# FFN of a hybrid encoder layer: first layer by seven block products of eight, second layer in blocks of four tiles

## The chip, the cores and the metric

One core of a Trainium2 chip runs the whole kernel. The metric is device time in microseconds, the median of several executions; one more execution was profiled. TensorE (PE) multiplies; PEld is its weight load; VectorE (DVE), ScalarE (ACT) and GpSimd (POOL) do elementwise work; SyncE (SP) and ACT issue most transfers.

## The reference

One step of an encoder layer over 1024 prompt tokens and 8 x 16 sample tokens, 1152 in all, with 1024 channels. Three mixers come first; the change touches only what follows them:

```python
h = _layer_norm(DN_ALPHA * x + merged @ w_out, ln1_g, ln1_b)
f = jnp.square(jax.nn.relu(h @ w_ff1 + b_ff1)) @ w_ff2 + b_ff2      # 1024 -> 4096 -> 1024
y = _layer_norm(DN_ALPHA * h + f, ln2_g, ln2_b)
```

## The kernel before

Every float32 operand of a product is split into a rounded part and a remainder (`split`, L168 on POOL, L169 on DVE), and each product is three matmuls: high by high, high by low, low by high. All matmuls are recorded at L115 and all transposes at L120, so operations are told apart by their tiles.

The channel-major activations stay in two tiles, `xh` and `xl`, of 8 channel slices by 1152 tokens (`hh`, `hl` in `phase_out`). In `phase_out` the attention output is multiplied by `w_out` into nine token tiles `acc` of 128 x 1024. Each is normalised (`layer_norm`, L1319 to L1330), transposed on PE in two halves (`tp`), and written back to `hh` and `hl` (L1252, L1253).

The FFN then runs over 32 tiles of 128 hidden channels, in 16 blocks of two. For each tile `f`, `weights` loads two raw halves of `w_ff1` and splits them. `gemm` makes 24 matmuls of 384 columns for each of three token chunks, into the two banks `g` of PSUM. ACT applies bias, Relu (L1274) and Square (L1275), and POOL and DVE split the result into `uh`, `ul`. Two raw halves of `w_ff2` are split into `h2`, `l2`. After a block's two tiles the second layer runs: for each of nine token tiles and two halves of the output, 6 matmuls of 512 columns into a bank `op` (tag `o`, three banks), added to `acc` by DVE (L1298, L1300; L1304 in the last block). Behind the last block's sum each token tile is normalised and stored (L1313).

The order of instructions on each engine is fixed when the program is built. A list scheduler takes, by priority in program order, what its own estimate says is ready; on the chip each engine then runs its list in order. Tiles of a pool with `bufs=n` rotate over n buffers, and a pool that opens where a closed one lay waits, tile by tile, for what lay there.

Of the kernel before, what the change touches and what calls it, by code (L numbers as in the profile page):

```python
# [2 lines left out]

# [1 line left out]

# [6 lines left out]
F32 = mybir.dt.float32  # L12
F32R = mybir.dt.float32r
AF = mybir.ActivationFunctionType
ALU = mybir.AluOpType
# [4 lines left out]
P = 128  # L20
D = 1024
# [3 lines left out]
NT = SEQ + DB * DT  # L25
# [32 lines left out]
def run(g, n=-1):  # L58

    while n and next(g, g) is not g:  # L60
        n -= 1


class K:
# [66 lines left out]
    def setup(self):  # L131
        nc, d = self.nc, self.d
        nc.scalar.preload_act_table_set("natural_log_exp_and_others")
        cst = self.const.tile([P, C_END], F32, name="cst")
        self.cst = cst
        self.ident = cst[:, C_ID:C_ID + P]
        self.og = self.dram.tile([KT, P, NT], F32, name="og")
        self.started = set()

        self.gates = [(0, 0), (0, 1), (0, 2), (0, 3), (1, 7)] + [(2, t) for t in range(4)] + [(a, t) for t in range(4, KT) for a in (0, 2)]  # L140
        self.oa, self.oc, self.gb = (self.dram.tile([KT, P, NT], F32, name=n) for n in ("oa", "oc", "gb"))
        self.spq = self.dram.tile([KT, P, NT], F32, name="spq")
# [1075 lines left out]
    def phase_out(self, pool, ps):  # L1218
        nc, d = self.nc, self.d
        T9 = NT // P  # L1220
        hh, hl = self.xh, self.xl
        accs = [pool.tile([P, D], F32, name=f"acc{i}") for i in range(T9)]
        with self.pool("p2a") as pa:
            for i in range(6):
                nc.scalar.copy(accs[i][:, 0:512], self.early[i])
                nc.sync.dma_start(accs[i][:, 512:D], d["x"][i][:, 512:D])
            for i in range(6, T9):
                t = slice(i * P, (i + 1) * P)
                mg = pa.tile([P, KT, P], F32, name="mg", bufs=1)
                nc.sync.dma_start(mg, self.og[:, :, t].rearrange("k p n -> p k n"))  # L1230
                nc.scalar.copy(hh[:, :, t], mg)
                nc.vector.tensor_sub(hl[:, :, t], mg, hh[:, :, t].bitcast(F32))
                nc.sync.dma_start(accs[i], d["x"][i])
                run(self.out_mm(i, 0, self.w0, self.psg.tile([P, 512], F32, name="ps", tag="g"), accs[i][:, 0:512]))
            lng = pa.tile([P, 2, D], F32, name="lng")
            for i, n in enumerate(("ln1_g", "ln1_b")):
# [17 lines left out]
        self.right.close()  # L1254
        with self.pool("p2b") as pb:
            bf = pb.tile([P, NF], F32, name="bf")
            nc.sync.dma_start(bf, d["b_ff1"])
            lng = pb.tile([P, 2, D], F32, name="lng")
            bf2 = pb.tile([P, D], F32, name="bf2")
            for t, n in ((bf2, "b_ff2"), (lng[:, 0, :], "ln2_g"), (lng[:, 1, :], "ln2_b")):  # L1260
                nc.sync.dma_start(t, d[n].broadcast_to([P, D]))
            blk = 2
            for f0 in range(0, NF, blk):
                hid = []
                for f in range(f0, f0 + blk):
                    w = self.weights(d["w_ff1"][f].rearrange("p (k c) -> p k c", k=KT))
                    uh = pb.tile([P, NT], F32R, name="uh", bufs=3)
                    ul = pb.tile([P, NT], F32R, name="ul", bufs=3)
                    for c in range(NCH):
                        n = slice(c * CW, (c + 1) * CW)  # L1270
                        p = self.psg.tile([P, 512], F32, name="ps", tag="g")
                        run(self.gemm(p[:, :CW], w, hh, hl, c * CW, (c + 1) * CW))
                        r = pb.tile([P, CW], F32, name="r", bufs=2)
                        nc.scalar.activation(r, p[:, :CW], AF.Relu, bias=bf[:, f:f + 1])  # L1274
                        nc.scalar.activation(r, r, AF.Square)  # L1275
                        self.split(uh[:, n], ul[:, n], r)
                    w2 = []
                    for u in range(2):
                        raw = pb.tile([P, 512], F32, name="w2raw", bufs=3)
                        nc.sync.dma_start(raw, d["w_ff2"][f][:, u * 512:(u + 1) * 512])  # L1280
                        h2 = pb.tile([P, 512], F32R, name="h2", bufs=6)
                        l2 = pb.tile([P, 512], F32R, name="l2", bufs=6)
                        self.split(h2, l2, raw)
                        w2.append((h2, l2))
                    hid.append((uh, ul, w2))
                last = f0 + blk == NF
                for i in range(T9):
                    t = slice(i * P, (i + 1) * P)
                    for u in range(2):
                        o = ps.tile([P, 512], F32, name="op", tag="o", bufs=3)  # L1290
                        m = 0
                        for uh, ul, w2 in hid:
                            for a, b in ((uh, w2[u][0]), (uh, w2[u][1]), (ul, w2[u][0])):
                                self.mm(o, lhsT=a[:, t], rhs=b, start=m == 0, stop=m == 3 * blk - 1)
                                m += 1
                        a = accs[i][:, u * 512:(u + 1) * 512]
                        if f0 == 0:
                            nc.vector.scalar_tensor_tensor(a, a, ALPHA, o, op0=ALU.mult, op1=ALU.add)  # L1298
                        elif not last:
                            nc.vector.tensor_add(a, o, a)  # L1300
                        else:
                            if u == 0:
                                sm = pb.tile([P, 2], F32, name="sm", bufs=2)
                            nc.vector.tensor_tensor_reduce(out=a, in0=o, in1=a, scale=1.0, scalar=0.0, op0=ALU.add, op1=ALU.add, accum_out=sm[:, u:u + 1])  # L1304
                    a = accs[i]
                    if f0 == blk:
                        nc.gpsimd.tensor_add(a, a, bf2)
                    if last:
                        self.layer_norm(pb, a, sm, lng, hl[:, :, t], i >= T9 - 2)
                        m = 2 if i >= T9 - 2 else 1  # L1310
                        for u in range(m):
                            v = slice(u * D // m, (u + 1) * D // m)
                            nc.sync.dma_start(d["o_y"][i][:, v], a[:, v])  # L1313

    def layer_norm(self, pool, a, s, gb, jk, short=False):

# [100 lines left out]
```

## Time and profile before

| | us |
|---|---|
| median of 3 executions | 2750.88 (2748.21 to 2756.87) |
| the profiled execution | 2752.38 |
| its span, first to last instruction | 2750.5 |
| FFN, first matmul of 384 columns to the end | about 1928 to 2750.5 |

In the rows, "mean ns" or min/median/max is the duration of one instruction. Matmuls overlap, so what one costs in a dense run is the distance from start to start. A row of the chain gives start, length and how many instructions were merged into it. A row of a timeline may end with the idle time before it and what ended it.

### The profile page before, as it was taken

The numbers are of one execution on the slowest core, as the hardware profiler recorded it, in microseconds if no ns is written. First come the engines' busy times: TensorE is split into PE (matmuls) and PEld (weight loads), VectorE is DVE, ScalarE is ACT, GpSimd is POOL, SyncE is SP. The second block draws the span as 40 slices with busy tenths as digits, with TensorE's granted clock in tenths as the row PEclk, the third lists the DMA queues.
The fourth block names the chain that finished last, engine by engine and source line by source line (L and its number), as shares of the span: only waits on it lengthen the run. The fifth ranks groups of instructions, "written<-read, shape, count | busy, mean of one in ns | idle before, by whom it ended". The sixth has DMA issues, their size and how long they took to land.

```text
span 2750.5 us, 45013 instructions
## 1 busy us (share of the span) xinstructions
PE 2655.3 (97%) x16361; PEld 2464.2 (90%) x16361; DVE 1448.3 (53%) x3353; ACT 1004.5 (37%) x2749; POOL 809.3 (29%) x1197
## 2 busy tenths in 40 slices
PE   8999999999999989999989989999999999999997
PEld 7989999999999989888888888878999999999996
DVE  4647484755647563333556666555444444444445
ACT  5646474655647453223433333234211111111113
POOL 2222222222222222212645555323251211211213
PEclk9999999999999999999999999999999999999999
DMA  6343434434343434444866766561210110110101
GB/s 224 104 153 120 163 123 149 148 125 164 114 150 120 163 124 148 164 155 153 252 180 199 211 196 185 175 218 47 79 57 31 54 39 31 54 39 31 61 20 69
DMA packets 263261, 343.27 MB, mean 125 GB/s; under 512 B 55408, under 2 KB 188160, under 8 KB 260480
## 3 DMA queue, kind: packets, MB, share of 16 engines
q1 hardware_dynamic: 201344, 245.93, 28.5%
q10 hardware_dynamic: 61696, 94.47, 10.0%
q8 instruction: 129, 2.11, 0.3%
q14 instruction: 92, 0.75, 0.1%
HBM read 267.69 MB, written 105.13 MB: 136 GB/s over the span
## 4 chain that ended last, share of the span: by engine, by line
PE 81%; DMA 8%; DVE 5%; issue 3%; POOL 2%; ACT 1%; SPq 0%; ACTq 0%; DVEq 0%; POOLq 0%
PE ps L115 48%; PE op L115 16%; PE od L115 3%; PE S L115 3%; PE t L115 2%; PE tb L120 2%; PE sc L115 1%; PE tp L120 1%; PE kk L115 1%; DMA bv<-spn 1%; DVE tmp L786 1%; PE o L115 1%; DMA wraw<-in_w_mem 1%; PE ob L115 1%; DMA kb<-in_cak 1%
## 5 line engine op out<-in xcount | busy, mean ns | idle before, releaser
L115 PE MATMUL ps<-xh,whi 128*128 128x384 f32 x2712 | 950.3, 350 | 10.3 <-POOL whi L168 7.0
L115 PE MATMUL ps<-xh,wlo 128*128 128x384 f32 x2712 | 927.6, 342 | 1.8 <-DVE wlo L169 1.8
L115 PE MATMUL ps<-xl,whi 128*128 128x384 f32 x2712 | 927.3, 342 | 0.0
L115 PEld LDWEIGHTS ps<-xh,whi 128*128 128x128 f32 x2712 | 511.2, 189 | 27.7 <-POOL whi L168 7.0
L115 PEld LDWEIGHTS ps<-xl,whi 128*128 128x128 f32 x2712 | 511.1, 188 | 16.5 <-issue 5.0
L115 PEld LDWEIGHTS ps<-xh,wlo 128*128 128x128 f32 x2712 | 510.2, 188 | 10.0 <-issue 2.5
L1300 DVE TENSOR_TENSOR acc<-op,acc 128x512 f32<-128x512 f32 x252 | 174.0, 691 | 276.2 <-PE op L115 276.1
L168 POOL TENSOR_SCALAR whi<-wraw 128x512 fp32r<-128x512 f32 x261 | 181.4, 695 | 458.2 <-PE ps L115 381.8
L1274 ACT ACTIVATE r<-ps,bf 128x384 f32<-128x384 f32 x96 | 55.6, 581 | 664.7 <-PE ps L115 659.7
L169 DVE TENSOR_TENSOR wlo<-wraw,whi 128x512 fp32r<-128x512 f32 x261 | 194.1, 744 | 163.2 <-POOL whi L168 161.2
L115 PE MATMUL op<-h,uh 128*128 128x512 f32 x576 | 225.6, 392 | 1.2 <-DVE sm L1304 1.2
L115 PE MATMUL op<-h,ul 128*128 128x512 f32 x576 | 226.1, 392 | 0.0
L115 PE MATMUL op<-l,uh 128*128 128x512 f32 x576 | 225.5, 392 | 0.0
L168 POOL TENSOR_SCALAR uh<-r 128x384 fp32r<-128x384 f32 x96 | 55.0, 573 | 491.8 <-ACT r L1275 479.9
L372 POOL TENSOR_SCALAR pt<-pt,sta 128x640 f32<-128x640 f32 (+3 forms) x144 | 111.3, 773 | 278.3 <-DVE sta L371 231.5
L618 DVE SCALAR_TENSOR_TENSOR y<-z,wc,y 128x384 f32<-128x384 f32 (+1 forms) x216 | 132.2, 612 | 28.2 <-ACT y L615 18.3
L115 PEld LDWEIGHTS op<-h,ul 128*128 128x128 f32 x576 | 108.2, 188 | 23.9
L115 PEld LDWEIGHTS op<-h,uh 128*128 128x128 f32 x576 | 108.3, 188 | 19.5 <-DVE sm L1304 2.0
L370 ACT ACTIVATE pt<-pt,sta 128x640 f32<-128x640 f32 (+3 forms) x144 | 101.0, 701 | 64.6 <-DVE sta L369 53.3
L115 PEld LDWEIGHTS op<-l,uh 128*128 128x128 f32 x576 | 108.1, 188 | 15.5
L368 DVE CUSTOM_DVE_ANT_0 pt<-S,tab 128x640 f32<-128x640 f32 (+4 forms) x128 | 83.7, 654 | 52.4 <-PE S L115 38.5
L169 DVE TENSOR_TENSOR ul<-r,uh 128x384 fp32r<-128x384 f32 x96 | 53.6, 560 | 102.0 <-POOL uh L168 102.0
(374 smaller groups left out, 4562.4 us busy)
## 6 DMA issues: line engine op xcount, KB each, us to landing
wraw<-in_w_in SPq DMA_DIRECT2D x160, 256.0 KB
kb<-in_cak SPq DMA_DIRECT2D x16, 1024.0 KB
vb<-in_cav SPq DMA_DIRECT2D x16, 1024.0 KB
wraw<-in_w_ff SPq DMA_DIRECT2D x64, 256.0 KB
w2raw<-in_w_ff SPq DMA_DIRECT2D x64, 256.0 KB
o_aks<-in_cak ACTq DMA_DIRECT2D x32, 496.0 KB
o_avs<-in_cav ACTq DMA_DIRECT2D x32, 496.0 KB
spn<-kn ACTq DMA_DIRECT2D x48, 192.0 KB
```

The lines of the kernel that those rows point to most:

```text
L115: ins = self.nc.tensor.matmul(out, **kw)
L120: ins = self.nc.tensor.transpose(out, **kw)
L168: nc.gpsimd.tensor_scalar(hi, raw, 1.0, 0.0, op0=ALU.mult, op1=ALU.add)
L169: nc.vector.tensor_sub(lo, raw, hi.bitcast(F32))
L368: nc.vector.tensor_tensor_reduce(out=P_, in0=S, in1=tab, scale=1.0, scalar=-3e38, op0=ALU.add, op1=ALU.max, accum_out=st[:, 0:1])
L370: nc.scalar.activation(P_, P_, AF.Exp, bias=st[:, 1:2], accum_out=st[:, 2:3])
L372: nc.gpsimd.tensor_scalar(P_, P_, st[:, 3:4], 0.0, op0=ALU.mult, op1=ALU.add)
L618: nc.vector.scalar_tensor_tensor(y[:, :w], z[:, i:i + w], wc[:, i:i + 1], y[:, :w], op0=ALU.mult, op1=ALU.add)
L786: nc.vector.tensor_tensor(tmp[:, 0:t, 0:t], y[:, 0:t, 0:t], m[:, 0:t, t].unsqueeze(1).broadcast_to([72, t, t]), op=ALU.mult)
L1274: nc.scalar.activation(r, p[:, :CW], AF.Relu, bias=bf[:, f:f + 1])
L1300: nc.vector.tensor_add(a, o, a)
```

## The change

The first four tiles of the first layer are computed as before, in four chunks of 288 columns instead of three of 384. The other 28 go in 14 pairs. For a pair, the tokens (two halves of 576), the input channels (two halves of four slices) and the two tiles form a 2 x 2 block product, which is made from seven block products instead of eight (Winograd's form). A product has 24 matmuls of 288 columns, in two banks. The sums of activations (S1 to S4) are made once by DVE and POOL from an unrounded copy `hm` and split by ACT and DVE; S3 takes the place of the upper half of `hh`. The sums of weights (t1 to t4) are made by POOL for each pair, and the products are added up by DVE out of PSUM. The PSUM banks rotate over three tags.

The hidden activations no longer stay on chip: each goes to DRAM (`hid`) and is read back by the second layer, which starts when the first is through, in 8 blocks of four tiles. Its `uh`, `ul` lie in the 8 slices of `xh`, `xl`. The nine `acc` also go to DRAM (`hd`) and come back. Raw weights of both layers share six buffers. `layer_norm` gets a scratch tile `jk`.

```diff
+        self.hd = self.dram.tile([NT // P, P, D], F32, name="hd")
+        self.hid = self.dram.tile([NF, 2, P, NT // 2], F32, name="hid")
...
+            hm = self.on_right("hm").tile([P, KT, NT], F32, name="hm")
...
+                nc.scalar.dma_start(self.hd[i], a)
...
                     nc.scalar.copy(hh[:, s, t], v)
+                    nc.scalar.copy(hm[:, s, t], v)
...
+        with self.pool("p2n") as pn:
+            raw = lambda: pn.tile([P, 512], F32, name="raw", bufs=6)
+            uraw = pn.tile([P, 2, NT], F32, name="uraw")
+            with self.pool("p2b") as pb:
+                self.ffn1(pb, ps, hm, raw)
+            self.right.close()
+            with self.pool("p2c") as pb:
+                self.ffn2(pb, ps, raw, uraw)
+    def ffn1(self, pool, ps, hm, raws):
+        bf = pool.tile([P, NF], F32, name="bf")
...
+        S = {i: tuple(pool.tile([P, 4, H], F32R, name=f"s{i}{n}") for n in "hl") for i in (2, 1, 4)}
+        S[3] = hh[:, top, two], hl[:, top, two]
+        names = cycle("gtogto")
...
+        def hidden(r, f, i):
+            nc.scalar.activation(r, r, AF.Relu, bias=bf[:, f:f + 1])
+            nc.scalar.activation(r, r, AF.Square)
+            nc.scalar.dma_start(self.hid[f, i], r)
...
+        for k in range(4):
+            a11, a21, a12, a22 = [hm[:, q, n] for q in (k, 4 + k) for n in (one, two)]
+            nc.vector.tensor_add(a22, a21, a22)
+            nc.gpsimd.tensor_sub(a21, a11, a21)
+            nc.vector.tensor_sub(a11, a22, a11)
+            self.cast(S[2], k, a11)
+            self.cast(S[1], k, a22)
+            self.cast(S[3], k, a21)
+            nc.vector.tensor_sub(a12, a12, a11)
+            self.cast(S[4], k, a12)
+        pool = self.on_right("p2r")
+        A11, A12, A22 = [(hh[:, q, n], hl[:, q, n]) for q, n in ((top, one), (low, one), (low, two))]
+        for f in range(4, NF, 2):
...
+            def product(a, raw):
+                w = [self.wp.tile([P, 4, P], F32R, name=n, tag=n, bufs=4) for n in ("whi", "wlo")]
+                self.split(*w, raw)
+                banks = []
+                for j in range(2):
+                    banks.append(bank())
+                    for k in range(4):
+                        for m, (x, y) in enumerate(((0, 0), (0, 1), (1, 0))):
+                            self.mm(banks[j], lhsT=w[x][:, k, :], rhs=a[y][:, k, half(j)], start=k == m == 0, stop=k == 3 and m == 2)
+                return banks
+            def add(x, banks):
+                y = keep()
+                for j in range(2):
+                    nc.vector.tensor_add(y[:, half(j)], banks[j], x[:, half(j)])
+                return y
+            p1 = keep()
+            for j, b in enumerate(product(A11, R[0, 0])):
+                nc.scalar.copy(p1[:, half(j)], b)
+            hidden(add(p1, product(A12, R[1, 0])), f, 0)
+            nc.gpsimd.tensor_sub(t1, R[0, 1], R[0, 0])
+            nc.gpsimd.tensor_sub(t2, R[1, 1], t1)
+            u2 = add(p1, product(S[2], t2))
+            u4 = add(u2, product(S[1], t1))
+            nc.gpsimd.tensor_sub(t4, R[1, 0], t2)
+            u5 = add(u2, product(A22, t4))
+            nc.gpsimd.tensor_sub(t3, R[1, 1], R[0, 1])
+            hidden(add(u4, product(S[4], R[1, 1])), f + 1, 0)
+            b = product(S[3], t3)
+            hidden(add(u5, b), f, 1)
+            hidden(add(u4, b), f + 1, 1)
+    def cast(self, pair, k, src):
+        self.nc.scalar.copy(pair[0][:, k, :], src)
+        self.nc.vector.tensor_sub(pair[1][:, k, :], src, pair[0][:, k, :].bitcast(F32))
+    def ffn2(self, pb, ps, raws, uraw):
+        blk = 4
+        for f0 in range(0, NF, blk):
+            for f in range(f0, f0 + blk):
+                raw = uraw[:, f % 2, :]
+                nc.sync.dma_start(raw.rearrange("p (i n) -> p i n", i=2), self.hid[f].rearrange("i p n -> p i n"))
+                uh, ul = self.xh[:, (f + 4) % 8, :], self.xl[:, (f + 4) % 8, :]
+                for c in range(NCH):
+                    n = slice(c * CW, (c + 1) * CW)
+                    self.split(uh[:, n], ul[:, n], raw[:, n], "act")
+                for u in range(2):
+                    raw = raws()
+                    nc.sync.dma_start(raw, d["w_ff2"][f][:, u * 512:(u + 1) * 512])
+                    h2 = pb.tile([P, 512], F32R, name="h2", bufs=12)
+                    l2 = pb.tile([P, 512], F32R, name="l2", bufs=12)
+                    self.split(h2, l2, raw)
...
+            if f0 == 0:
+                accs = [pb.tile([P, D], F32, name=f"acc{i}") for i in range(T9)]
...
+                for i in range(T9):
+                    nc.sync.dma_start(accs[i], self.hd[i])
```

What follows in `ffn2` (a block's matmuls for each token tile and half, now 12 over four tiles where it was 6 over two, the sum into `acc`, the last block's `layer_norm` and stores) has the text of before.

## Rows read from the trace of the kernel before

**Rows 1.** Page, part 1: busy us, share of the span, instructions of each engine.
```profile
PE 2655.3 (97%) x16361; PEld 2464.2 (90%) x16361; DVE 1448.3 (53%) x3353; ACT 1004.5 (37%) x2749; POOL 809.3 (29%) x1197
```

**Rows 2.** Windows (busy of PE, PEld, DVE, ACT, POOL; clock; DMA share; GB/s): block, last block, tail.
```profile
2142.67:2192.91 50.24, 50.24 (x253) 45.70 (x253) 21.96 (x33) 6.63 (x12) 9.65 (x15) 1.00 0.13 42
...
2710.14:2736.30 26.16, 24.98 (x109) 19.78 (x107) 22.89 (x45) 17.97 (x36) 12.81 (x6) 1.00 0.22 89
2736.30:2750.48 14.18, 0.11 (x1) 0.00 (x0) 10.09 (x15) 4.95 (x10) 5.01 (x2) 0.64 0.43 169
```

**Rows 3.** Chain that ended last (start, us, what), FFN: both kinds of matmul.
```profile
2142.67 14.84 PE ps L115 x84
2157.51 4.10 PE op L115 x18
```

**Rows 4.** Timeline of PE, two stretches of narrower matmuls (start us, us, instruction).
```profile
139.87 0.31 PE L115 MATMUL S<-kd,qs 128*128 128x320 f32 x1
...
140.44 0.28 PE L115 MATMUL od<-pth,vv 128*128 128x256 f32 x1
...
1127.52 0.36 PE L115 MATMUL ps<-memh,whi 128*128 128x256 f32 x1
1127.72 0.28 PE L115 MATMUL ps<-meml,whi 128*128 128x256 f32 x1
...
1138.92 0.28 PE L115 MATMUL ps<-memh,wlo 128*128 128x256 f32 x1
```

**Rows 5.** Tile memh: weight loads of 256-column matmuls (ns min/median/max).
```profile
L115 PEld LDWEIGHTS ps<-memh,whi x128: 187/190/194, 1070.0 to 1253.6; 128*128 128x128 f32 x128
```

**Rows 6.** Groups by shape, whole span: DVE, POOL and ACT operations nearest the new ones.
```profile
L169 DVE TENSOR_TENSOR l<-w2raw,h 128x512 fp32r<-128x512 f32 x64 | 56.9, 910 | 12.2 <-POOL h L168 12.2
L169 DVE TENSOR_TENSOR ul<-r,uh 128x384 fp32r<-128x384 f32 x96 | 53.6, 560 | 102.0 <-POOL uh L168 102.0
L833 DVE TENSOR_TENSOR at<-kk,E 128x256 f32<-128x256 f32 x24 | 10.1, 422 | 20.4 <-PE kk L115 20.4
...
L168 POOL TENSOR_SCALAR h<-w2raw 128x512 fp32r<-128x512 f32 x64 | 49.7, 778 | 70.9 <-PE op L115 46.5 <-DMA w2raw<-in_w_ff 23.2
L991 POOL TENSOR_TENSOR we<-wv,cst 128x512 f32<-128x512 f32 x16 | 18.1, 1133 | 3.4 <-DMA o_ssmp<-S 1.7 <-ACT wv L979 1.2 <-PE kk L115 0.4
...
L1275 ACT ACTIVATE r<-r 128x384 f32<-128x384 f32 x96 | 50.3, 525 | 2.9
```

**Rows 7.** Timeline of ACT in the first normalisation.
```profile
1916.14 1.15 ACT L1320 ACTIVATE xl<-acc,lst 128x1024 fp32r<-128x1024 f32 x1 [2.31 <-issue]
```

**Rows 8.** Tile acc on DVE, last 51 us (ns min/median/max, first and last start).
```profile
L1304 DVE CUSTOM_DVE_ANT_0 acc<-op,acc x18: 673/680/692, 2711.6 to 2738.5; 128x512 f32<-128x512 f32 x18
L1321 DVE SCALAR_TENSOR_TENSOR acc<-acc,lst,lng x9: 1272/1286/3196, 2715.2 to 2743.3; 128x1024 f32<-128x1024 f32 x9
L1327 DVE SCALAR_TENSOR_TENSOR acc<-acc,lst,lng x4: 737/739/740, 2744.5 to 2746.5; 128x512 f32<-128x512 f32 x4
```

**Rows 9.** Timeline of the tail: PE's last matmul, ACT, and SP's stores.
```profile
2736.02 0.39 PE L115 MATMUL op<-h,ul 128*128 128x512 f32 x1
...
2740.08 1.13 ACT L1320 ACTIVATE xl<-acc,lst 128x1024 fp32r<-128x1024 f32 x1
...
2741.21 0.47 ACT L1322 ACTIVATE lst<-lst,eps 128x1 f32<-128x1 f32 x2
...
2740.04 7.56 SPq L1313 DMA_DIRECT2D o_y<-acc  x6
```

**Rows 10.** Timeline: a 512 KB load issued by SP, and ACT's first read of it.
```profile
1842.73 0.38 SPq L1230 DMA_DIRECT2D mg<-og  x1
...
1846.92 1.04 ACT L1231 CAST xh<-mg 128x1024 fp32r<-128x1024 f32 x1
```

**Rows 11.** Page, part 2: GB/s in 40 slices of the span.
```profile
GB/s 224 104 153 120 163 123 149 148 125 164 114 150 120 163 124 148 164 155 153 252 180 199 211 196 185 175 218 47 79 57 31 54 39 31 54 39 31 61 20 69
```

More of the change, by code (lines that the diff above doesn't have):

```diff
@@ L1 @@
 from contextlib import ExitStack, contextmanager
-from itertools import chain
+from itertools import chain, cycle
 import numpy as np
@@ L1221, in phase_out @@
         hh, hl = self.xh, self.xl
-        accs = [pool.tile([P, D], F32, name=f"acc{i}") for i in range(T9)]
         with self.pool("p2a") as pa:
+            accs = [pa.tile([P, D], F32, name=f"acc{i}") for i in range(T9)]
             for i in range(6):
@@ L1252, in phase_out @@
                     nc.scalar.copy(hh[:, s, t], v)
+                    nc.scalar.copy(hm[:, s, t], v)
                     nc.vector.tensor_sub(hl[:, s, t], v, hh[:, s, t].bitcast(F32))
[L1254 to L1286, printed above, removed]
-                for i in range(T9):
[L1288 to L1313, printed above, removed]
@@ new lines, in phase_out, with bank @@
+        with self.pool("p2n") as pn:
[7 more added lines that the diff above has]
+    def ffn1(self, pool, ps, hm, raws):
+        nc, d = self.nc, self.d
+        hh, hl = self.xh, self.xl
+        H = NT // 2
+        bf = pool.tile([P, NF], F32, name="bf")
+        nc.sync.dma_start(bf, d["b_ff1"])
+        one, two = slice(0, H), slice(H, NT)
+        top, low = slice(0, 4), slice(4, 8)
+        S = {i: tuple(pool.tile([P, 4, H], F32R, name=f"s{i}{n}") for n in "hl") for i in (2, 1, 4)}
+        S[3] = hh[:, top, two], hl[:, top, two]
+        names = cycle("gtogto")
+        def bank():
+            tag = next(names)
+            if tag == "g":
+                return self.psg.tile([P, 512], F32, name="ps", tag="g")[:, 0:288]
+            return ps.tile([P, 512], F32, name=tag + "p", tag=tag, bufs={"t": 2, "o": 3}[tag])[:, 0:288]
+        def hidden(r, f, i):
+            nc.scalar.activation(r, r, AF.Relu, bias=bf[:, f:f + 1])
+            nc.scalar.activation(r, r, AF.Square)
+            nc.scalar.dma_start(self.hid[f, i], r)
+        res = lambda: pool.tile([P, H], F32, name="r", bufs=3)
+        for f in range(4):
+            w = self.weights(d["w_ff1"][f].rearrange("p (k c) -> p k c", k=KT))
+            for i in range(2):
+                r = res()
+                for j in range(2):
+                    p = bank()
+                    run(self.gemm(p, w, hh, hl, (2 * i + j) * 288, (2 * i + j + 1) * 288))
+                    u = r[:, j * 288:(j + 1) * 288]
+                    nc.scalar.activation(u, p, AF.Relu, bias=bf[:, f:f + 1])
+                nc.scalar.activation(r, r, AF.Square)
+                nc.scalar.dma_start(self.hid[f, i], r)
+        for k in range(4):
[11 more added lines that the diff above has]
+        for f in range(4, NF, 2):
+            R = {}
+            for g in range(2):
+                src = d["w_ff1"][f + g].rearrange("p (k c) -> p k c", k=KT)
+                for q in range(2):
+                    R[q, g] = raws().rearrange("p (k c) -> p k c", k=4)
+                    nc.sync.dma_start(R[q, g], src[:, 4 * q:4 * q + 4, :])
+            t1, t2, t3, t4 = (pool.tile([P, 4, P], F32, name="tsum", bufs=6) for _ in range(4))
+            half = lambda j: slice(288 * j, 288 * j + 288)
+            keep = lambda: pool.tile([P, H], F32, name="keep", bufs=5)
+            def product(a, raw):
[10 more added lines that the diff above has]
+                y = keep()
+                for j in range(2):
+                    nc.vector.tensor_add(y[:, half(j)], banks[j], x[:, half(j)])
[15 more added lines that the diff above has]
+            hidden(add(u4, b), f + 1, 1)
```

38 lines of the change are left out of this document (added).

## The prediction

> **What bounds the kernel now.** I read the busy times first. TensorE is busy 97% of the span, DVE 53%, POOL 29% [rows 1], but a share of busy time over the span says little of one stage, so next came windows of the FFN. In a block of two hidden tiles PE is busy 50.24 of 50.24 us at the full granted clock (1.00, the 2.4 GHz level), while DVE works 22 us, POOL 10 and ACT 7 [rows 2]. The chain of waits agrees: through the FFN it is matmuls alone, one after the other [rows 3]. So here a matmul removed is time removed, and the other engines have more than half of their time free. From the chain come the prices of a matmul in a dense run: 14.84/84 = 176.7 ns at 384 columns and 4.10/18 = 227.8 ns at 512 [rows 3]. A block is 144 x 0.1767 + 108 x 0.2278 = 50.05 us, so the rows leave 0.2 us of it unexplained. Only the end is different. In the last block PE has matmuls in flight for 24.98 of 26.16 us, and after its last one come 14.2 us in which DVE, ACT, POOL and a store end the program [rows 2].
>
> **The seven products.** Before, a pair of hidden tiles costs 144 x 0.1767 = 25.44 us. After, it has 7 x 24 = 168 matmuls of 288 columns, a shape that the trace doesn't show. The nearest rows on either side are 256 columns, where a dense run goes from 1127.72 to 1138.92, 94 steps of 119 ns, and 320 columns, four in 0.57 us, 143 ns each [rows 4]. These are the bounds: between 119 and 143 ns. A line from 119 at 256 to 176.7 at 384 gives 148 at 320, so it is some 5 too high there, and 133.4 at 288; halfway between the two bounds is 131. I take 133, near the line, since its operands are those of the 384-column run. A pair then costs 168 x 0.133 = 22.34 us, 3.10 less, and 14 pairs save **43.4 us**. The bounds for it are 14 x (25.44 - 168 x 0.119) = 76 and 14 x (25.44 - 168 x 0.143) = 20. An eighth of the 356 us of these pairs would be 44.5; narrower matmuls carry a larger fixed part.
> The Trainium skill, "TensorE: Matmul & The Clock Gate", section "Back-to-back issue gap", puts a single warm gap at N/2.4 + 2.5 ns, 122.5 ns for 288 columns. By that the pairs would save 14 x (25.44 - 20.58) = 68 us. The row of 384 columns is 176.7 where the same rule says 162.5, so the row decides.
>
> The first four tiles keep their columns in four chunks: 384 x 0.133 = 51.07 us against 288 x 0.1767 = 50.89, **+0.2 us**. The second layer has the same 1728 matmuls of 512 columns, so nothing changes on PE; its DVE sums halve in number, which are off the path.
>
> **What the other engines get in a pair of 22.3 us.** DVE: seven remainders at up to 0.910, and 14 sums of 288 columns from PSUM at about 0.455 (between 0.422 at 256 and 0.560 at 384): 12.7 us. POOL: seven roundings at 0.778 and four weight sums at 1.133: 10.0 us. ACT: eight passes over 576 columns at about 0.71 (from 0.525 at 384 [rows 6] and 1.15 at 1024 [rows 7]), two copies and four transfers to issue at some 0.4 each: 7.3 us [rows 6]. All is hidden by PE. Uncovered, DVE's work beyond today's would be the dearest. Weight tiles have four buffers and products use six banks in turn, so PE can be three products (9.6 us) ahead of what empties them. Transfers: a pair loads 1.05 MB and stores 1.18, 100 GB/s; a second-layer block of 49.2 us loads 4.5 MB, 90 GB/s. Earlier slices of the span move up to 252 [rows 11]. I cost them at nothing.
>
> **Making the sums of activations.** Per channel slice DVE has three sums and four remainders of 576 columns (about 0.8 each, by 0.560 at 384): 22 us for four slices; ACT 16 casts at 0.71, 11 us; POOL four differences at about 1.3. They start when the last token tile is transposed and are hidden by the 51 us of the first four tiles. S3 alone must wait until those have read the upper half of `hh`. It then takes four casts and four remainders, pipelined some 4 us, and the weight sums lie where `hm` lay, so POOL's t1 and t2 (2.3 us) and a split (1.7) come behind: 8 us against two products (6.4 us) that PE can do before the third. In `phase_out` each token tile gives ACT two more copies (0.6 each) and a transfer that waits for POOL's last sum; behind it stand the next tile's Square and copies. ACT idles 2.31 us per tile there [rows 7], so 1.6 fits; if it doesn't, PE has tiles 0 to 3 of earlier tokens to go on with. For all this **+1 us**, bounds 0 and 8.
>
> **The turn from the first layer to the second.** It didn't exist before, since the layers alternated. Call T the end of the last product. The second layer's first four tiles go into the lower slices of `xh`, free for good after the fifth product, at T - 6.3. The hidden tiles come through two buffers, so the third can only be loaded when the first is split (two more chunks on ACT and DVE, about 1.6 us, T - 4.7). A load of 0.5 MB takes 4.2 us from issue to use [rows 10], and one more split 1.1: T + 0.6 for tile three, about T + 2 for tile four, where PE wants them at T + 1.4 and T + 2.1. Also, the first `h2` lies where the bias `bf` and S2 lay, and `bf` is read by the last Relu: two DVE sums, then ACT, then a split, about T + 4. PE can do the other output half first if the list has it so. The nine `acc` come back behind on SP's queue; the first sum needs one at about T + 4. I take **+3 us**. Below: 0, all covered. Above: all four tiles split after T, one load and 12 x 0.56 + 8 x 0.91, 18 us.
>
> **The tail.** Before, the last block gives a token tile 2.73 us of PE, while DVE needs two sums (0.76 each with the read of the sum), 0.2 and 1.27 to 3.2 us for the fused normalisation; the last two of the nine queue up [rows 8]. From PE's last start at 2736.02 to 2750.5 are 14.5 us. After, a tile has 5.47 us of PE, so DVE keeps up. What is left behind the last matmul: 0.4 to its end, 0.76 + 0.4, Square and its read 1.3, two small passes 0.5, two halves at 0.74, and 3.2 for the last store (from 2747.3, the last half's end, to 2750.5): 8.0 us [rows 8, 9]. With 1.3 us of stall inside the last block (26.16 against 108 x 0.2278 = 24.6 and the last one's end): **-7.7 us**, bounds -9 and -4.
>
> **Sum.** 2752.4 (the profiled execution, 1.5 above the median of the runs and within them) - 43.4 + 0.2 + 1 + 3 - 7.7 = 2705.5. I forecast **2705 us**.
>
> **The rivals.**
> *The turn is serial.* If the list has the splits in an order that the chip can't use, the upper bound above holds, 15 us more: 2715 to 2725. For it speaks that two hidden buffers and `bf` tie the start to the end of the first layer; against it, that the first chunks are free at T - 16.
> *Products wait.* A matmul whose group had to wait shows 200 ns to the next one instead of 119 (from 1127.52) [rows 4]. If every half product began so, 196 x 0.08 = 16 us; if each product also waited 0.3 us for a weight or a bank, 98 x 0.3 = 29 more: 2721 to 2750. DVE can be slowed by POOL: the same normalisation took 1.27 and 3.2 us [rows 8]. If DVE were lengthened by all of POOL's four sums, 12.7 + 4.5 = 17.2 us, still under 22.3. So waits would come from order, not from load. From 0.5 us per product the gain is gone.
> *Weight loads bind.* This one ends slower. PEld is busy 45.7 of 50.24 us of a block [rows 2], 91%, and the change raises the loads: 276 instead of 252 per pair of tiles over both layers, and 96 more in the first four. If a load's slot of 50.24/252 = 0.199 us set the pace, 14 x 24 + 96 = 432 loads more are 86 us: 2835. It decides from 151 ns per matmul of 288 columns, where a pair costs what it did. Against it: loads of 187 to 194 ns each [rows 5] run beside 256-column matmuls that start every 119 ns [rows 4], so loads overlap one another.
> The Trainium skill, "Perfetto Trace Analysis", section "Identifying the Most-Contended Engine", judges TensorE's headroom by the busy share of LDWEIGHTS; by it the loads are nearly full here, and 2835 would be the time. The 256-column rows speak against.
>
> **How the numbers follow.** Chances: forecast 0.70, serial turn 0.10, products wait 0.15, loads bind 0.05. A time within 0.3% (8 us) of before is what a measurement of this kernel can't tell from no change. The first two are faster; of the third 0.07 ends below 2743, 0.05 in between, 0.03 above; the fourth is slower. So faster 0.87, same 0.05, slower 0.08. The forecast's own range: the line was about 5 ns off at 320 columns, and 6 ns on 2352 + 384 matmuls is 16 us either way, 2689 to 2721. The serial turn and the milder waits add the stretch up to 2730. So 2689 to 2730.
>
> **What would show it.** Right: matmuls of 288 columns start 130 to 136 ns apart with no idle PE between products; 22 to 23 us per pair; a hole of 0 to 5 us where the layers meet; about 8 us from the last matmul to the end. Wrong: steps of 140 ns or more; idle PE before product groups put down to POOL or DVE; a hole of over 10 us at the turn, or a lower clock behind it; a second layer with gaps where a block begins.

## The result, and the profile after

The changed kernel takes 2714.14 us (median, 2710.72 to 2718.88, four executions), the kernel before, run beside it, 2753.88. The ratio is 0.987 (95% interval 0.9853 to 0.9886): 1.3% faster, 36 us by the ratio (31 to 40). The forecast was 2705, with a range from 2689 to 2730. The profiled execution took 2710.72 us with a span of 2708.9.

Busy times, page of the kernel after, part 1, the line that answers to [rows 1]. PE has 432 matmuls more and is busy 48 us less:

```profile
PE 2607.6 (96%) x16793; PEld 2418.9 (89%) x16793; DVE 1494.4 (55%) x3475; ACT 1063.6 (39%) x2851; POOL 866.9 (32%) x1203
```

Windows of the kernel after, columns as in [rows 2]: more than eleven pairs of the seven products; the turn between the layers; a stretch of the third second-layer block; 49 us of a later block; the tail from the last matmul's start.

```profile
2016.12:2275.69 259.57, 259.57 (x1958) 259.57 (x1958) 128.97 (x247) 74.15 (x122) 108.56 (x124) 1.00 0.29 101
...
2286.70:2303.50 16.80, 4.53 (x10) 2.86 (x10) 11.70 (x22) 9.17 (x19) 4.84 (x6) 0.63 0.91 305
...
2409.50:2418.00 8.50, 5.20 (x16) 3.83 (x15) 6.54 (x13) 1.29 (x3) 0.05 (x1) 0.80 0.81 254
...
2463.00:2512.00 49.00, 49.00 (x218) 40.56 (x217) 25.03 (x38) 5.96 (x13) 6.89 (x8) 1.00 0.29 93
...
2700.40:2708.90 8.50, 0.34 (x2) 0.00 (x0) 4.00 (x7) 1.74 (x4) 0.00 (x0) 0.72 0.33 124
```

In the products PE is busy 259.57 of 259.57 us at clock 1.00: 259.57/1958 = 132.6 ns a matmul. The last block and its tail [rows 2] took 26.16 + 14.18 us; from the last matmul's start to the end it is now 8.6. New are two holes, in the second and third window, where PE works 4.53 of 16.80 and 5.20 of 8.50 us, at mean granted clocks of 0.63 and 0.80. The chain of waits, start, length and what, is matmuls alone in the products and in a later block (as in [rows 3]), and at the turn it leaves PE:

```profile
2016.12 1.58 PE ps L115 x12
2017.70 1.60 PE tp L115 x12
2019.30 1.58 PE op L115 x12
...
2280.42 3.65 DMA uraw<-hid
...
2286.16 3.76 DMA uraw<-hid
...
2290.48 2.34 DVE xl L171 x3
...
2292.84 5.26 DMA uraw<-hid
...
2298.12 0.52 ACT xh L166
...
2298.66 1.50 DVE xl L171 x3
2300.16 0.61 DVE l L171
...
2300.79 6.59 DMA raw<-in_w_ff
...
2307.45 0.62 POOL h L170
...
2439.85 60.29 PE op L115 x266
...
2700.88 0.60 DVE acc L1416
...
2701.84 1.25 ACT jk L1432 x2
...
2703.11 1.30 DVE acc L1433
...
2704.50 0.75 DVE acc L1439
2705.25 0.66 DVEq L1519
```

How long each stage took, by the starts of its matmuls (PE's timeline, first and last of each shape), in us:

| stage | before | after |
|---|---|---|
| `phase_out` from the first `op<-woh` matmul to the FFN's first | 1862.0 to 1927.6: 65.6 | 1851.9 to 1917.5: 65.6 |
| FFN, first matmul to the start of the last | 808.4 | 782.8 |
| the last matmul's start to the end | 14.5 | 8.6 |
| together | 888.5 | 857.0 |

The part that the change touches became 31.5 us shorter. The two profiled executions differ by 41.7: the other 10 us lie ahead of `phase_out`, in instructions that the change leaves as they were. In eleven more executions, of this kernel and of variants, `phase_out` begins between 1859.7 and 1870.9, so 1851.9 was an early one. All stage times below count from a matmul, which leaves this out.

Pure matmuls explain most of it: before 16 x 25.44 + 1728 x 0.2278 = 800.6, after (2352 + 384) x 0.133 + 393.6 = 757.5. That is 43.1 less. What exceeds the pure matmuls grew from 7.8 to 25.3 us. After, 5.2 of it are in the first layer and 20.3 in the second (counted to the last matmul's end, 0.2 more), of which 16.2 lie in its first block, 5.0 in its third, and nearly nothing in the others.

Where the 16.2 come from is seen in PE's timeline at the turn, kernel after (a bracket holds the idle time before, and what ended it):

```profile
2286.53 0.29 PE L115 MATMUL tp<-xh,wlo 128*128 128x288 f32 x1
2290.58 0.50 PE L115 MATMUL op<-h,xh 128*128 128x512 f32 x1 [3.76 <-POOL h L170]
...
2291.57 1.22 PE L115 MATMUL op<-h,xh 128*128 128x512 f32 x2 [0.49 <-POOL h L170]
...
2300.82 0.80 PE L115 MATMUL op<-l,xh 128*128 128x512 f32 x1 [8.02 <-DVE l L171]
2301.41 0.63 PE L115 MATMUL op<-h,xl 128*128 128x512 f32 x1
2301.84 0.63 PE L115 MATMUL op<-h,xh 128*128 128x512 f32 x1
```

Two waits, for the first rounded weight `h` and for the first remainder `l`. Behind the second, matmuls start 427 ns apart instead of 227, at a granted clock of 0.50 (the 1.2 GHz level), which lasts until 2304.8; the 0.63 above is the mean of both levels. A window inside that stretch:

```profile
2301.40:2303.50 2.10, 2.10 (x6) 1.67 (x5) 2.10 (x5) 0.29 (x1) 0.00 (x0) 0.50 1.02 419
```

POOL's and DVE's timelines of the same kernel say why each was late:

```profile
2289.91 4.84 POOL L170 TENSOR_SCALAR h<-raw 128x512 fp32r<-128x512 f32 x6 [15.24 <-ACT keep L1290]
```

```profile
2298.66 1.50 DVE L171 TENSOR_TENSOR xl<-uraw,xh 128x384 fp32r<-128x384 f32 x3 [3.04 <-ACT xh L166]
2300.08 1.89 DVE L171 TENSOR_TENSOR l<-raw,h 128x512 fp32r<-128x512 f32 x3
```

The six `h` come in one row behind 15.24 idle us, released by the last Relu (L1290), which reads the bias whose place they take. The first `l` starts 10 us after its `h`, although nothing but DVE is needed: in DVE's list the splits of hidden tiles 0 to 6 stand ahead of it (21 `xl`). Tiles 2, 4 and 6 come one behind the other into the same one of the two buffers, by loads of 3.65, 3.76 and 5.26 us in the chain.

### The profile page after: what moved, and what is told of

The parts are those of the page before. It is cut to its first block, busy times and chain, and to the rows that moved or that the text cites. A ratio compares the mean times of both kernels' runs of the same rounds, so it can differ in the third digit from the quotient of the medians.

```text
span 2708.9 us, 46387 instructions
## 1 busy us (share of the span) xinstructions
PE 2607.6 (96%) x16793; PEld 2418.9 (89%) x16793; DVE 1494.4 (55%) x3475; ACT 1063.6 (39%) x2851; POOL 866.9 (32%) x1203
## 3 DMA queue, kind: packets, MB, share of 16 engines
q10 hardware_dynamic: 72208, 118.06, 12.5%
## 4 chain that ended last, share of the span: by engine, by line
PE 78%; DMA 9%; DVE 6%; issue 3%; ACT 1%; POOL 1%; SPq 0%; DVEq 0%; ACTq 0%; POOLq 0%
PE ps L115 38%; PE op L115 19%; PE tp L115 4%; PE od L115 3%; PE S L115 3%; PE t L115 2%; PE tb L120 2%; PE sc L115 1%; DVE tmp L788 1%; PE tp L120 1%; PE kk L115 1%; DMA bv<-spn 1%; PE o L115 1%; DMA wraw<-in_w_mem 1%; DMA uraw<-hid 1%
## 5 line engine op out<-in xcount | busy, mean ns | idle before, releaser
L115 PE MATMUL ps<-xh,whi 128*128 128x384 f32 (+2 forms) x2144 | 749.0, 349 | 10.3 <-POOL whi L170 7.4
L115 PE MATMUL ps<-xh,wlo 128*128 128x384 f32 (+2 forms) x2144 | 726.7, 339 | 1.4 <-DVE wlo L171 1.4
L115 PE MATMUL ps<-xl,whi 128*128 128x384 f32 (+2 forms) x2144 | 725.8, 339 | 0.0
L115 PEld LDWEIGHTS ps<-xh,whi 128*128 128x128 f32 (+1 forms) x2144 | 404.2, 189 | 22.7 <-POOL whi L170 7.6
L115 PEld LDWEIGHTS ps<-xl,whi 128*128 128x128 f32 (+1 forms) x2144 | 404.4, 189 | 9.0 <-issue 5.0
L115 PEld LDWEIGHTS ps<-xh,wlo 128*128 128x128 f32 (+1 forms) x2144 | 403.5, 188 | 6.8 <-issue 2.5
L115 PE MATMUL op<-l,xh 128*128 128x512 f32 x576 | 225.7, 392 | 8.0 <-DVE l L171 8.0
L115 PE MATMUL op<-h,xh 128*128 128x512 f32 x576 | 225.2, 394 | 8.3 <-POOL h L170 4.7
L115 PE MATMUL op<-h,xl 128*128 128x512 f32 x576 | 225.4, 391 | 0.0
L620 DVE SCALAR_TENSOR_TENSOR y<-z,wc,y 128x384 f32<-128x384 f32 (+1 forms) x216 | 132.8, 615 | 28.4 <-ACT y L617 18.8
L115 PEld LDWEIGHTS op<-l,xh 128*128 128x128 f32 x576 | 109.1, 189 | 31.5 <-DVE l L171 8.7
L1290 ACT ACTIVATE keep<-keep,bf 128x576 f32<-128x576 f32 x56 | 42.0, 774 | 211.2 <-DVE keep L1343 211.2
```

The lines of the kernel that those rows point to most:

```text
L115: ins = self.nc.tensor.matmul(out, **kw)
L620: nc.vector.scalar_tensor_tensor(y[:, :w], z[:, i:i + w], wc[:, i:i + 1], y[:, :w], op0=ALU.mult, op1=ALU.add)
L1290: nc.scalar.activation(r, r, AF.Relu, bias=bf[:, f:f + 1])
```

## The experiments

Stage times are from one profiled execution each. Except for e3 the first layer repeats to 0.2 us in all eleven; the second layer of the same kernel differs by 2.0 us between two. "First layer" is the time from the first 288-column matmul's start to the last one's, and one step more. "Loss" is the second layer, from the end of the last 288-column matmul to that of the last 512-column one, less 393.6. The FFN's time is from the first 288-column matmul to the end of the span.

| kernel | time, us | ratio to before, 95% | first layer | loss | of it block 1, 2, 3 | FFN |
|---|---|---|---|---|---|---|
| after | 2714.14 | 0.9870 (0.9853 to 0.9886) | 369.1 | 20.3 | 16.2, 0.4, 5.0 | 791.4 |
| e0_after | 2716.70 | 0.9879 (0.9842 to 0.9915) | 369.1 | 22.3 | 16.3, 0.5, 6.2 | 793.4 |
| e1_bias_apart | 2727.66 | 0.9906 (0.9886 to 0.9926) | 369.1 | 28.4 | 16.7, 1.0, 5.8 | 799.5 |
| e2_raw8 | 2721.34 | 0.9883 (0.9867 to 0.9899) | 369.1 | 19.1 | 14.4, 0.4, 5.6 | 790.2 |
| e3_plain | 2757.43 | 1.0020 (1.0004 to 1.0037) | 412.3 | 18.0 | 13.6, 0.7, 5.0 | 832.2 |
| e4_blk2 | 2741.14 | 0.9958 (0.9943 to 0.9973) | 369.2 | 33.6 | 18.3, 6.5, 1.8 | 811.6 |
| e5_remainders | 2719.58 | 0.9887 (0.9841 to 0.9932) | 369.1 | 19.6 | 14.5, 0.3, 6.1 | 790.8 |
| e6_rem_bias | 2717.87 | 0.9878 (0.9844 to 0.9912) | 369.1 | 16.9 | 5.2, 1.0, 5.7 | 788.0 |
| e7_spread | 2718.23 | 0.9884 (0.9846 to 0.9922) | 369.1 | 17.6 | 16.2, 0.1, -0.2 | 788.7 |
| e8_all | 2706.62 | 0.9822 (0.9808 to 0.9836) | 369.3 | 5.5 | 4.5, 0.4, -0.2 | 776.7 |
| e9_shift | 2713.43 | 0.9851 (0.9829 to 0.9873) | 369.1 | 13.4 | 4.3, 1.0, 1.0 | 784.5 |
| e10_half | 2704.98 (one execution) | | 369.3 | 6.6 | 5.9, 0.2, -0.2 | 777.9 |

For e4 a column of blocks is a pair of its blocks of two tiles.

**e3_plain: the first layer without the seven products.** All 32 tiles go as the first four do; the sums, the products and their additions are left out.

```diff
-        for f in range(4):
+        for f in range(NF):
...
-        for k in range(4):
-            a11, a21, a12, a22 = [hm[:, q, n] for q in (k, 4 + k) for n in (one, two)]
...
-            hidden(add(u4, b), f + 1, 1)
```

> All 32 tiles of the first layer by eight products of eight, in four chunks of 288 columns, as the first four are made now; hidden tiles through DRAM, second layer in blocks of four as in the changed kernel. It parts the seven products from the rest. Theory (the seven products are worth 14 x 3.1 = 43 us): the first layer takes 3072 x 0.133 = 408.6 us from its first to its last matmul instead of 369, and the time is about 2714 + 40 to 43, 2755. Rival (the products also bring waits of their own, or the gain comes from the last block and from elsewhere): first layer under 395 us, time under 2740.

The first layer takes 412.3 us instead of 369.1, so the seven products are worth 43.2. Its window has 2338.33 - 1926.21 us for 3098 recorded matmuls, again 133 ns each:

```profile
1926.21:2338.33 412.12, 411.04 (x3098) 410.12 (x3097) 51.32 (x77) 119.45 (x215) 40.82 (x62) 1.00 0.27 92
```

That compares with eight products of the same 288 columns and contains the sums; in the prediction's own terms, against 384 columns, 132.6 ns give 14 x (25.44 - 168 x 0.1326) = 44.3. Without the seven products the kernel is no faster than before (its FFN takes 832.2 us where before's took 822.9): the gain of the whole change is theirs, and what the other parts win at the end, 5.9 us, is less than what they lose at the turn and in the third block.

**e4_blk2: blocks of two tiles in the second layer.**

```diff
-        blk = 4
+        blk = 2
```

> The second layer in blocks of two hidden tiles, as before the change, with all else as changed. Theory (blocks of four are worth 6 to 8 us at the end, since a token tile has 5.47 us of matmuls instead of 2.73, and cost at the turn, since the first block needs four tiles): from the last matmul to the end 14 us again instead of 8.3, but the turn loses 8 to 12 us less; time within 5 us of 2714. Rival (the block size doesn't matter at the end): 8 us at the end, time about 2705.

The tail grows from 8.6 to 15.4 us, near before's 14.5: it is the longer last block that shortened it. Window from the start of the last matmul:

```profile
2721.90:2737.30 15.40, 0.40 (x2) 0.00 (x0) 11.47 (x16) 5.48 (x11) 5.01 (x2) 0.59 0.44 171
```

The turn became no shorter (PE's two waits there are 3.98 and 7.82 us), so it isn't the four tiles' weights that PE waits for. The 8 to 12 us that were expected back there didn't come, and the time is 2741 instead of about 2714: besides the tail, each block of two now has a wait of some 0.6 us for the sum into `acc`, 1.0 with what follows it, and the second pair of blocks loses 6.5.

**e1_bias_apart: the bias outside the place of the first `h2`.** The first theory (A): the Relu that reads `bf` holds POOL's splits back, and these the turn.

```diff
             uraw = pn.tile([P, 2, NT], F32, name="uraw")
+            bf = pn.tile([P, NF], F32, name="bf")
...
-                self.ffn1(pb, ps, hm, raw)
+                self.ffn1(pb, ps, hm, raw, bf)
...
-        bf = pool.tile([P, NF], F32, name="bf")
```

> The 128 bytes of bias of the first layer are kept in a place of their own, so the first split of second-layer weights no longer lies over them; nothing else is changed. In the changed kernel POOL starts its six splits only when the last Relu has read the bias (2289.9), and the second layer loses 20.4 us against its 393.6 us of matmuls. Theory A (the bias holds POOL's list, and everything at the turn is late behind it): the splits start 10 us or more earlier, the loss falls to about 8 us, the time to about 2702. Theory B (the six raw buffers and the transfers queued on SP set the turn: the last two raw halves are loaded late whatever POOL does): the splits move, the loss stays within 5 us of 20, the time within 2709 to 2717.

This execution is 11 us later than after's all the way from `phase_out`, and its products end at 2298.0; POOL begins to split the six `h` 12 us ahead of that. POOL and then DVE, timelines of e1_bias_apart:

```profile
2286.00 0.63 POOL L170 TENSOR_SCALAR h<-raw 128x512 fp32r<-128x512 f32 x1
...
2288.74 3.86 POOL L170 TENSOR_SCALAR h<-raw 128x512 fp32r<-128x512 f32 x5 [2.11 <-PE tp L115]
```

```profile
2309.24 1.50 DVE L171 TENSOR_TENSOR xl<-uraw,xh 128x384 fp32r<-128x384 f32 x3 [2.51 <-ACT xh L166]
2310.65 1.89 DVE L171 TENSOR_TENSOR l<-raw,h 128x512 fp32r<-128x512 f32 x3
```

PE's wait for `h` is gone and the one for the first `l` is 12.5 us: the turn costs 16.7 where it cost 16.2. So A falls: the bias was the first of two gates, and with it opened PE stands at the second. The whole loss, 28.4, fits neither theory, for the kernel became slower elsewhere: every 512-column matmul takes 232.4 instead of 226.7 ns (below, e9).

**e2_raw8: eight raw buffers instead of six.** The rival: the raw weights of the last tiles come too late. Room for two more buffers is made by letting the square's scratch lie in `uraw`.

```diff
-            raw = lambda: pn.tile([P, 512], F32, name="raw", bufs=6)
+            raw = lambda: pn.tile([P, 512], F32, name="raw", bufs=8)
...
-                jk = pb.tile([P, KT, P], F32, name="jk")
...
-                    self.layer_norm(pb, a, sm, lng, jk, i >= T9 - 2)
+                    self.layer_norm(pb, a, sm, lng, uraw[:, 0, 0:D].rearrange("p (k n) -> p k n", k=KT), i >= T9 - 2)
```

> Eight raw buffers instead of six, so all eight raw halves of the first second-layer block can be loaded before the turn; the scratch of the last normalisation goes into the buffer of the hidden tiles to make room. Theory A (bias holds POOL): POOL still starts at the last Relu, so the first wait of about 4 us stays, but eight splits then run in a row; the loss of the second layer falls from 20 to about 12 us, the time to 2706. Theory B (raw buffers): the wait of 8.7 us for a remainder and the one for the last raw halves are gone, loss about 6 us, time about 2700. If hidden tiles with their two buffers set it, loss stays near 20.

POOL now splits eight halves in a row, again behind the Relu:

```profile
2302.79 6.49 POOL L170 TENSOR_SCALAR h<-raw 128x512 fp32r<-128x512 f32 x8 [15.42 <-ACT keep L1290]
```

The waits of 3.9 and 7.6 us stay (3.76 and 8.02 in after), and only the later, short one for the fourth tile's weights goes: 14.4 for 16.2. The whole loss, 19.1, is near the 20 that the expectation gives to the hidden tiles' two buffers. The raw buffers are a part, not the cause.

**e5_remainders: the first weight remainders ahead of later hidden splits.** The third theory (C): DVE's order. An edge in the program's order, without a wait, puts the splits of hidden tiles 4 to 7 behind the remainder of tile 3's weights.

```diff
+                    x = self.split(uh[:, n], ul[:, n], raw[:, n], "act")
+                    if 4 <= f < 8:
+                        self.behind(x, ls[3])
```

> One ordering edge: on DVE the hidden tiles of the second block are split behind the second-layer weights of the first block. In the changed kernel DVE's list has the splits of hidden tiles 0 to 6 ahead of the first remainder of those weights, and tile 6 comes by the fifth of a chain of loads through two buffers. Theory C (DVE's list makes the turn: the remainder waits for hidden loads that the first block doesn't need): the wait of 8.7 us before the second matmul goes to under 2 us, and the second layer loses 10 to 13 us instead of 20.4. Theory D (the raw weights are late whatever the list: six buffers, loads queued behind hidden tiles and accumulators): the remainders move, the wait moves to the fourth tile's weights, and the loss stays above 17.

Only 14.5 for 16.2. The wait moved: the chain of e5_remainders now runs through the raw load for the fourth tile, which can start only when DVE has read a raw buffer, and then takes 9.61 us. It is issued behind four of the nine accumulators, and the whole loss is 19.6, which is what the rival D said:

```profile
2299.21 1.10 DVE l L171
...
2300.32 9.61 DMA raw<-in_w_ff
...
2310.00 0.63 POOL h L170
```

**e6_rem_bias: both gates.** The bias apart as in e1, and each hidden split from tile 2 on behind the remainder two tiles before.

```diff
+                    if 2 <= f < 8:
+                        self.behind(x, ls[f - 2])
```

> Both: the bias in a place of its own, and on DVE the hidden tile f behind the second-layer weights of tile f-2 in the first two blocks. Theory C: POOL's splits are done early, the remainders follow, PE goes on within 3 us of the last product and then waits only for the fourth tile; the second layer loses 6 to 10 us. With the bias alone it lost 28. Theory D: loss stays above 17, with the wait at the fourth tile's weights, which are loaded behind four accumulators.

The first block's loss falls to 5.2: PE's timeline of e6_rem_bias has waits of 0.82 and 1.75 us where after had 3.76 and 8.02.

```profile
2298.44 0.86 PE L115 MATMUL op<-h,xh 128*128 128x512 f32 x3
...
2300.12 0.50 PE L115 MATMUL op<-l,xh 128*128 128x512 f32 x1 [0.82 <-DVE l L171]
...
2309.21 0.50 PE L115 MATMUL op<-h,xh 128*128 128x512 f32 x1 [1.75 <-POOL h L170]
```

So C holds together with the bias: e1 alone made the turn 0.5 us longer and e5 alone 1.7 shorter, both gates opened take 11 off it (e6's order without the bias's move wasn't run, nor more buffers for hidden tiles, which is the other way to free DVE's list). The whole loss, 16.9, isn't the 6 to 10 of theory C: the hole of the third block is still there, and each block pays 1.0 us for the bias's new place again, as in e1.

**e7_spread: the output bias in blocks two to six.** In after, POOL adds `bf2` to all nine accumulators behind the second block, 2.39 us each, and the splits of later weights stand among the last of them. POOL, kernel after, then DVE, where a remainder that takes 0.63 elsewhere takes 2.87 us beside such a sum, then PE, which waits for a sum into `acc` that comes behind the remainders in DVE's list:

```profile
2397.73 2.39 POOL L1419 TENSOR_TENSOR acc<-acc,bf 128x1024 f32<-128x1024 f32 x1
2400.09 5.44 POOL L170 TENSOR_SCALAR h<-raw 128x512 fp32r<-128x512 f32 x6
```

```profile
2397.80 2.87 DVE L171 TENSOR_TENSOR l<-raw,h 128x512 fp32r<-128x512 f32 x1 [0.76 <-POOL h L170]
```

```profile
2413.22 0.50 PE L115 MATMUL op<-h,xh 128*128 128x512 f32 x1 [3.31 <-DVE acc L1412]
```

The rest of the third block's 5.0 us goes to the matmuls behind that wait, where the granted clock is 0.50 for 3.4 us.

```diff
-                if f0 == blk:
+                if f0 == blk * (1 + i // 2):
                     nc.gpsimd.tensor_add(a, a, bf2)
```

> The output bias is added by POOL to two token tiles in each of blocks 1 to 5 instead of to all nine in block 1. Theory (nine sums of 2.4 us in one block hold up POOL's splits of the next block's weights, and PE waits 3.7 us and some more at a lower clock where block 2 begins): that wait is under 0.5 us, the second layer loses 5 us less than 20.4; time about 5 us less than the changed kernel run beside it. Rival (the wait comes from raw buffers or loads): it stays.

The hole of the third block is gone, from 5.0 and 6.2 to -0.2. The whole time doesn't show it (2718.23 us beside e0's 2716.70, with wide intervals); the FFN does, 788.7 for 793.4. A hole of 1.8 is new in block six, where PE waits for a bank. The ninth sum isn't its cause, since it comes at 2622.93, long after. As in the kernel after, a sum ahead of the hole (here the eighth, at the end of block five) stands on POOL between the first split of the next weights and six more, and DVE's remainder beside it takes 2.88 us. POOL, then PE, of e7_spread:

```profile
2563.34 2.40 POOL L1419 TENSOR_TENSOR acc<-acc,bf 128x1024 f32<-128x1024 f32 x1
...
2577.23 0.50 PE L115 MATMUL op<-h,xh 128*128 128x512 f32 x1 [1.71 <-DVE acc L1412]
```

**e0_after: the changed kernel again, beside these.**

> The changed kernel once more. Its profiled execution reached the output projection at 1851.9 us, four variants with the same instructions up to there at 1860 to 1865, and the kernel before at 1862.0. Theory (executions differ in the mixers by some 10 us, and the first profile was an early one): 1858 to 1866 this time, time 2714 to 2722. Rival (the placement of this kernel's buffers in DRAM makes its mixers faster): 1850 to 1854 again.

The FFN takes 793.4 us where the first profile had 791.4, and `phase_out` begins at 1863.5 instead of 1851.9. From there to the end are 859.0 us, 29.5 less than before: so some 30 us is the size of the change in the part that it touches, and the rest of the first pair's 41.7 lay ahead of it. The ratios of whole executions say 36 us (31 to 40) and, here, 33 (23 to 43); what makes the first of them higher isn't shown.

**e8_all: everything that helped, with the bias in a tile of 2048 bytes.** Edits of e2, e6 and e7 (the ninth output-bias sum on DVE), and:

```diff
+            bf = pn.tile([P, 512], F32, name="bf")[:, 0:NF]
```

> All that helped, together: the order of remainders on DVE, eight raw buffers, the output bias over five blocks (the last token tile's by DVE), and the bias of the first layer apart, but in a place of 2 KB, so that all that lies behind it moves by 2048 bytes instead of 128. Theory C for the turn: first block loses under 4 us, third block none. Theory E (moving the second-layer buffers by 128 bytes made their matmuls of 512 columns 232.4 ns instead of 226.7): 226.7 again. The stage from the first matmul of 288 columns to the end, 791 to 793 us in the changed kernel, comes to about 773 to 776, the time to about 2699.

2706.62 us, 0.9822 of before (0.9808 to 0.9836): faster than both kernels. The loss falls from 20.3 and 22.3 to 5.5: 4.5 at the turn and 1.8 in block six, less 0.2 in most of the others. That is a little above the expected 4 at the turn, 773 to 776 for the FFN and 2699 in all. The hole of block six stays with the ninth sum on DVE, which fits: the eighth is where it was in e7. At the turn PE is busy 29.91 of 33 us at the full clock, while the queues move 344 GB/s:

```profile
2297.00:2330.00 33.00, 29.91 (x128) 23.05 (x127) 20.33 (x35) 7.46 (x16) 3.29 (x4) 1.00 0.98 344
...
2463.00:2512.00 49.00, 49.00 (x218) 40.58 (x217) 25.09 (x39) 5.78 (x12) 11.65 (x10) 1.00 0.29 91
```

**e9_shift and e10_half: the same with 128 and with 1024 bytes.** The instructions of e9 have the order of e8 on every engine; what lies behind the bias has other addresses.

```diff
-            bf = pn.tile([P, 512], F32, name="bf")[:, 0:NF]
+            bf = pn.tile([P, 32], F32, name="bf")[:, 0:NF]
```

In e10_half the 512 is 256.

> As e8, with the bias in a place of 128 bytes: the same instructions in the same order on each engine, only the addresses behind it differ. Theory E (addresses): matmuls of 512 columns at 232 ns, 1728 x 5.7 = 10 us more than e8 in the second layer, 785 us for the stage. Rival (the slower matmuls came from other order or from more work beside them): 226.7 ns, same time as e8.

> As e8, with a place of 1024 bytes. Theory E says nothing on which distances count; if only multiples of the 2048 bytes of a weight buffer are fast, 232 ns, if smaller ones do too, 226.7.

The chain from 2440 on, first of e8_all, then of e9_shift, is dense in both, 60.29/266 = 226.7 and 60.19/259 = 232.4 ns:

```profile
2439.91 60.29 PE op L115 x266
```

```profile
2439.89 60.19 PE op L115 x259
```

e10_half, of one execution, has e8's row, 60.29 us for 266. So 128 bytes cost 5.7 ns on each of 1728 matmuls, 9.8 us by that, of which the FFN's times show 784.5 - 776.7 = 7.8; 1024 and 2048 bytes cost nothing.

## Why the prediction was right, and where its terms were off

**The seven products were sized right.** 132.6 ns a matmul, 133 taken; 43.2 us measured by e3 (44.3 against 384 columns), 43.4 forecast. No PE time was lost between products: the rival in which products wait, and the one in which weight loads set the pace, didn't happen. The latter is plainest in the window of the products: PEld is busy for all of the 259.57 us, and the matmuls still start every 133 ns. Loads allow a shorter step than that: matmuls of 256 columns start every 119 ns beside loads of 187 to 194 ns [rows 4, 5]. The rule of the Trainium skill ("Perfetto Trace Analysis", section "Identifying the Most-Contended Engine") reads TensorE's headroom from the share of peak FLOPs and the busy share of the loads; here a busy share of 100% didn't set the pace. The 122.5 ns of the Trainium skill's rule for a single matmul ("TensorE: Matmul & The Clock Gate", section "Back-to-back issue gap") are 10 ns short of the row.

**The cover held.** In the products DVE worked 50% and POOL 42% of the time (the forecast's 12.7 and 10.0 of 22.3 us were 57% and 45%; its 7.3 for ACT leaves out the two copies that it names, 8.1 with them, which changed nothing), and the transfers moved 101 GB/s where 100 was estimated; in a block of the second layer 93 for 90. `phase_out` has the same 65.6 us from its first matmul to the FFN's. The sums of activations cost about the 1 us given to them: PE is busy 13.93 of 15.00 us while DVE makes them, and e3, which has no such sums, lacks this wait.

```profile
1935.00:1950.00 15.00, 13.93 (x105) 13.69 (x104) 15.00 (x16) 8.70 (x15) 8.33 (x6) 1.00 0.17 57
```

**The tail.** -7.7 was forecast. From the last matmul's start 5.9 us went, and the 1.3 of stall inside the last block: -7.2. e4 gives back the first of these with the small block.

**The turn was the term that failed.** "I take +3 us", with an upper bound of 18: it was 16.2. The forecast saw the bias as a gate ("about T + 4") and the third hidden tile's load. It has no wait for the first remainders in its +3; the list has 21 splits of hidden tiles ahead of them, and these follow loads through two buffers. This is the rival of the serial turn in mechanism and nearly in size, to which 0.10 was given. In the waits the clock fell too, to 0.50 for 13.7 us; the 3.76, 0.49 and 8.02 us of idle PE are 12.3 of the 16.2, and most of the rest are matmuls at the lower clock behind them.

**The third block was not foreseen.** The prediction has no term for the bias sums on POOL; what it calls "off the path" are DVE's sums into `acc`. It reckoned with DVE slowed by POOL (1.27 and 3.2 us, [rows 8]), but in the products alone. Nine bias sums in one place cost 5.0 to 6.2 us, shown by e7.

By these, 43.1 less and 17.5 more in the FFN and 5.9 less behind it are the 31.5 less that the stages show, where the prediction had 46.9. The profiled execution came within 5.2 us of the 2705.5 only because its mixers were 10 us early; the median, 2714, is 9 off.

**What was luck.** The range was right with two terms wrong. Its 16 us either way were worked out for the price of a matmul, which was met; they happened to have room for the 15.4 us by which the stages fall short of the 46.9, 13 at the turn among them and 5 in the third block. Three of the prediction's own signs of being wrong came: a hole of over 10 us at the turn, a lower clock behind it, and a gap where a block begins.

**What stays open.** Why the shift of 128 bytes slows matmuls: e9 moved everything behind the bias at once, and which operand matters wasn't separated. Of e8's remaining 4.5 us at the turn and 1.8 in block six no cause was tried. For the first, the chain of e8 leads through a load of a hidden tile of 11.66 us, whose splits stand in DVE's list ahead of a sum into `acc` that PE waits 1.73 us for; for the second, the eighth bias sum at the end of block five is the likely one, and no run moved it.

## What to carry to other kernels

Seven block products of eight pay nearly their full eighth where PE is the bound and the narrower matmul keeps its price per column (here 133 ns at 288 against 176.7 at 384). Where two phases meet, read the lists of the in-order engines, since a gate opened alone (e1, e5) only shows the next one; and put side work that has a whole phase to be done in, such as bias sums, into several blocks (and, as the eighth sum suggests, not to a block's end). Halving the number of blocks made the end 7 us shorter, by giving the other engines more time for each last tile.

## What the hardware showed that was not expected

Moving the second layer's buffers by 128 bytes raised a 512-column matmul from 226.7 to 232.4 ns, in three kernels (e1, e6, e9); 1024 and 2048 bytes left it at 226.7 (e10, e8). Behind a hole of 8 us, eight matmuls of 512 columns started 427 ns apart at a granted clock of 0.50, where 227 ns is the price at 1.00. Loads of hidden tiles that took 3.65 us in the chain before the turn took 5.26 in the middle of it, at 305 GB/s, and 11.66 in e8's, at 344:

```profile
2309.83 11.66 DMA uraw<-hid
```
